# The order of the last pair's products in a fused QKV projection, and its last block stored in two halves

## The chip, the cores and the metric

The kernel runs on one core of a Trainium2 chip. The metric is the device time of one execution in microseconds; the figure given is the median of several runs. A profiled execution has a time of its own and a span, which goes from its first to its last instruction.

## What is computed

The reference multiplies a batch of activations by one weight matrix and splits the result into three parts, all in float32:

```python
batch, seq, hidden = 16, 512, 768
qkv = np.matmul(x, w_qkv)          # x (16, 512, 768), w_qkv (768, 2304)
q = qkv[..., :hidden]; k = qkv[..., hidden:2*hidden]; v = qkv[..., 2*hidden:]
return np.stack([q, k, v], axis=0).astype(np.float32)
```

So 8192 rows of x times 2304 columns of w, with 768 as the inner dimension. The output is 75.5 MB.

## The kernel before

**Tiles.** The 8192 rows are worked in 32 groups of 256 rows, two row blocks of 128 each (a group is `p`, and NP is 32). The 2304 columns are four blocks of 512 and a remainder of 256 (`CB`, `REM`). Two column blocks and two row blocks make a "quad": a 2 by 2 arrangement of 128x512 output blocks c11, c12, c21, c22. Quad `a` of a group has the first two column blocks (`q` is 0), quad `b` the last two (`q` is 1); the remainder columns lie between them, at 1024 to 1279, and belong to the middle third of the output.

**Products.** A quad is not computed as eight half products (two row blocks, two column blocks, two halves of the inner dimension) but as seven, by the Winograd form of Strassen's algorithm. Each product is three matmuls of 128x128 by 128x512 (line 258, in `product`). Products 1 and 2 use x and w rounded to bfloat16; products 3 to 7 use sums of blocks of x (made by GpSimd, `sums_x`) and of w (made once). In this text a6 is product 6 of quad a, and so on.

**Banks and readers.** A product is summed into a PSUM bank, and the block that it contributes to is read from there. The order inside `do` matters here:

- product 1 goes into bank x, and ScalarE copies it to c11 (line 267);
- product 2 goes into bank z, and VectorE adds it to c11 (line 280);
- product 6 is summed on top of product 1 in bank x, and ScalarE copies the sum to c12 (line 286);
- product 5 goes into bank y, and in the last group ScalarE copies it to c22 (line 291);
- product 7 is summed on top in bank x, and in the last group VectorE adds the sum to c22 (line 295);
- product 4 is summed on top in bank x, and ScalarE copies the sum to c21 (line 301);
- product 3 is summed on top in bank y, and VectorE adds the sum to c12 (line 304).

So products 6, 7 and 4 must each wait until the reader of the former sum in bank x is done, and product 3 until the reader of bank y is. A block is complete, and can be stored, after product 2 (c11), 7 (c22), 4 (c21) and 3 (c12).

**The remainder.** One row block of the 256 remainder columns is six matmuls of 128x128 by 128x256 (line 321, `rem_row`). In the last group, `rem_stored` makes one row block, copies its first 128 columns with ScalarE (line 423) and its other 128 with VectorE (line 424), and issues its store from ScalarE's DMA queue (line 426). In this text r0 and r1 are the remainders of the last group's two row blocks.

**Order.** The schedule is written out by hand: each engine executes its instructions in the order in which the program issues them (`manual_schedule`), and the semaphores between engines follow from the data. After a start-up in which the weights are loaded, rounded and summed, groups are worked two by two in the loop at the end of the kernel; the last group stands alone in `last`, which is where the change is made. Stores go to the DMA queue of SP, apart from the remainder's and one block (c21 of quad a), which go to ScalarE's. `store_cols` (line 416) stores one 128x512 block, 256 KB; where a block crosses from one third of the output to another, it is still one transfer.

Of the kernel before, what the change touches and what calls it, by code (L numbers as in the profile page):

```python
# [10 lines left out]
def kernel(  # L11
# [20 lines left out]
    nc = tc.nc  # L32
# [10 lines left out]
    CB = 512  # L43
    REM = N3 - 4 * CB
# [5 lines left out]
    ident = mybir.ActivationFunctionType.Identity  # L50
    add = mybir.AluOpType.add
# [188 lines left out]
    def quad(p, q, pool=o_pool, tag="o"):  # L240
        u = Quad()
        u.p, u.q = p, q
        u.o = pool.tile([P, 2, 2 * CB], fp32, name="o", tag=tag)
        u.x = u.y = u.z = None
        return u

    def product(u, n, ps, start):
        t1, t2, t3, t4 = ts[u.q]
        if n <= 2:
            h = (n - 1) * KH  # L250
            lhs = [xb[u.p][:, h + j, :P] for j in range(KH)]
            rhs = [b1[u.q][:, h + j, :] for j in range(KH)]
        else:
            k, t = {3: (4, b22[u.q][:]), 4: (0, t4), 5: (1, t1), 6: (2, t2), 7: (3, t3)}[n]
            lhs = [sr[u.p][:, k, j, :] for j in range(KH)]
            rhs = [t[:, j, :] for j in range(KH)]
        for j in range(KH):
            nc.tensor.matmul(  # L258
                ps[:], lhs[j], rhs[j],
                start=(start and j == 0), stop=(j == KH - 1), skip_group_check=True,  # L260
            )

    def bank():
        return ps_pool.tile([P, CB], fp32, name="ps")

    def evacuate(u):
        nc.scalar.activation(u.o[:, 0, :CB], u.x[:], ident)

    def do(u, n, out=True):
        c11, c12 = u.o[:, 0, :CB], u.o[:, 0, CB:]  # L270
        c21, c22 = u.o[:, 1, :CB], u.o[:, 1, CB:]
        if n == 1:
            u.x = bank()
            product(u, 1, u.x, True)
            if out:
                evacuate(u)
        elif n == 2:
            u.z = bank()
            product(u, 2, u.z, True)
            nc.vector.tensor_tensor(c11, c11, u.z[:], op=add)  # L280
        elif n == 6:
            first = u.x is None
            if first:
                u.x = bank()
            product(u, 6, u.x, first)
            nc.scalar.activation(c12, u.x[:], ident)  # L286
        elif n == 5:
            u.y = bank()
            product(u, 5, u.y, True)
            if u.p == NP - 1:  # L290
                nc.scalar.activation(c22, u.y[:], ident)
        elif n == 7:
            product(u, 7, u.x, False)
            if u.p == NP - 1:
                nc.vector.tensor_tensor(c22, c22, u.x[:], op=add)
            else:
                nc.scalar.activation(c22, u.x[:], ident)  # L297
                nc.vector.tensor_tensor(c22, c22, u.y[:], op=add)  # L298
        elif n == 4:
            product(u, 4, u.x, False)  # L300
            nc.scalar.activation(c21, u.x[:], ident)  # L301
        elif n == 3:
            product(u, 3, u.y, False)
            nc.vector.tensor_tensor(c12, c12, u.y[:], op=add)  # L304
# [14 lines left out]
    def rem_row(p, r, ps):  # L319
        for j in range(KT):  # L320
            nc.tensor.matmul(  # L321
                ps, xb[p][:, j, r * P:(r + 1) * P], w_rem[j // KH][:, j % KH, :],
                start=(j == 0), stop=(j == KT - 1), skip_group_check=True,
            )
# [77 lines left out]
    def store_cols(u, r, lo, hi, eng):  # L402

        c = Q_OFF[u.q] + lo
        n = hi - lo
        row = (2 * u.p + r) * P
        src = u.o[:, r, lo:hi]
        left = (c // H + 1) * H - c
        if left >= n:
            dst = out_flat[c // H, row:row + P, c % H:c % H + n]  # L410
        else:
            assert 2 * left == n
            first = out_flat[c // H, row:row + P, c % H:H]
            dst = bass.AP(first.tensor, first.offset, [[H, P], [M * H - H + left, 2], [1, left]])
            src = src.rearrange("m (s n) -> m s n", s=2)
        eng.dma_start(dst, src)

    def rem_stored(p, r):
        ps = bank()
        rem_row(p, r, ps[:, :REM])  # L420
        o = or_pool.tile([P, 2, REM], fp32, name="orem")
        half = REM // 2
        nc.scalar.activation(o[:, 0, :half], ps[:, :half], ident)  # L423
        nc.vector.tensor_copy(out=o[:, 0, half:], in_=ps[:, half:REM])  # L424
        row = (2 * p + r) * P
        nc.scalar.dma_start(out_flat[1, row:row + P, R_OFF - H:R_OFF - H + REM], o[:, 0, :])

    def last(a, b):

        do(a, 1)  # L430
        do(b, 1)
        rem_stored(a.p, 0)
        for u in (a, b):
            do(u, 2)
            store_cols(u, 0, 0, CB, nc.sync)
        do(a, 6)
        do(b, 6)
        for u in (a, b):
            do(u, 5)
            do(u, 7)  # L440
            store_cols(u, 1, CB, 2 * CB, nc.sync)
        for u in (a, b):
            do(u, 4)
            store_cols(u, 1, 0, CB, nc.scalar if u is a else nc.sync)
            do(u, 3)
            store_cols(u, 0, CB, 2 * CB, nc.sync)
        rem_stored(a.p, 1)


# [130 lines left out]
    u = quad(2, 0)  # L580
# [72 lines left out]
    for p in range(ND + 3, NP - 1, 2):  # L653
# [14 lines left out]
        a, b = quad(p, 0), quad(p, 1)  # L668
# [3 lines left out]
        plain(a, b, c, d, early, lambda: rem(c.p)()(), final)  # L672
        summed(c, d, {} if final else {0: lambda: transpose(p + 3, 2, 0)}, "parts" if final else True)
    last(quad(NP - 1, 0), quad(NP - 1, 1))


# [28 lines left out]
```

## Time and profile before

| | us |
|---|---|
| Median of 3 runs | 359.17 (358.98 to 359.32) |
| Profiled execution, its own time | 358.81 |
| Its span, first to last instruction | 357.0 |
| TensorE busy in the span | 350.6 |
| First matmul of the last group's stage in the record | 343.00 |
| End of the last matmul | 353.69 |
| Last store issued | 354.35 |

The remaining 1.81 us of the profiled execution's time lie outside its span. Engines are named PE (TensorE's matmuls), PEld (TensorE's weight loads), DVE (VectorE), ACT (ScalarE), POOL (GpSimd) and SP (which issues DMAs). Lines such as L304 are lines of the kernel. A line of the timeline has the start, the length, the engine, the line, the operation, what is written and read, the shapes and the number of instructions merged, and in brackets the idle time ahead of it with what ended that. The matmuls are pipelined, so the lengths of neighbours overlap; the distance between starts is what one costs. SPq and ACTq are the DMA queues of SP and ScalarE.

### The profile page before, as it was taken

Reading aid. Unit: us, or ns where it says so; the run is one execution under the profiler, and the core shown is the slowest. Engines: PE = TensorE matmul, PEld = TensorE weight load, DVE = VectorE, ACT = ScalarE, POOL = GpSimd, SP = SyncE. Lnnn points to the kernel's source line nnn. Section 1 sums busy time; section 2 is a strip of 40 time slices with the busy share of each in tenths; the row PEclk is TensorE's granted clock in tenths of the full one; section 3 lists DMA queues with packets and bytes.
Section 4 is the critical chain, followed back from the end, with each engine's and each line's share of the span. In section 5 each row is a group of like instructions: output and inputs, shape, how many; then the busy total and the mean of one; then the engine's idle time right before and its main releaser. Section 6 shows DMA issues by size and latency. Waiting matters only on the chain.

```text
span 357.0 us, 5315 instructions
## 1 busy us (share of the span) xinstructions
PE 350.6 (98%) x1757; PEld 252.1 (71%) x1776; DVE 264.4 (74%) x310; ACT 185.0 (52%) x317; POOL 177.3 (50%) x184
## 2 busy tenths in 40 slices
PE   7999999999999999999999999999999999999996
PEld 3474677768677686877768677686877768677674
DVE  3789876796877869777695877869777695876743
ACT  4587754545454553645545454553645545454553
POOL 0031773376566453665535566353665535566320
PEclk9999999999999999999999999999999999999999
DMA  7997999999999898998979899698999979887497
GB/s 296 380 353 238 325 378 340 373 317 348 308 311 340 257 361 206 347 266 285 361 197 385 227 342 307 209 402 213 347 263 307 331 196 392 225 303 280 155 380 260
DMA packets 82075, 108.10 MB, mean 303 GB/s; under 512 B 4992, under 2 KB 62080, under 8 KB 82048
## 3 DMA queue, kind: packets, MB, share of 16 engines
q1 hardware_dynamic: 75088, 102.52, 85.7%
q10 hardware_dynamic: 6960, 5.24, 5.5%
q8 instruction: 14, 0.23, 0.3%
q14 instruction: 13, 0.11, 0.1%
HBM read 32.24 MB, written 75.50 MB: 302 GB/s over the span
## 4 chain that ended last, share of the span: by engine, by line
PE 74%; POOL 15%; DVE 6%; issue 3%; DMA 2%; ACT 0%; SPq 0%
PE ps L258 56%; PE ps L321 12%; PE ps L496 6%; DVE xf L155 6%; POOL xb L205 5%; POOL s L226 3%; POOL s L225 3%; POOL s L227 3%; DMA xin<-in_x_dram 2%; PE ps L185 0%; DVE o L304 0%; ACT xc L166 0%; SPq L162 0%; DVE orem L424 0%; ACT orem L423 0%
## 5 line engine op out<-in xcount | busy, mean ns | idle before, releaser
L258 PE MATMUL ps<-t,s 128*128 128x512 f32 x720 | 177.9, 395 | 0.0
L258 PEld LDWEIGHTS ps<-t,s 128*128 128x128 f32 x720 | 135.1, 188 | 29.5
L155 DVE STREAM_TRANSPOSE xf<-xin 128x768 f32<-128x768 f32 (+1 forms) x45 | 93.3, 2075 | 4.3 <-DMA xin<-in_x_dram 4.3
L258 PE MATMUL ps<-b,xb 128*128 128x512 bf16 x343 | 81.6, 379 | 1.1
L298 DVE TENSOR_TENSOR o<-o,ps 128x512 f32<-128x512 f32 x56 | 38.5, 688 | 50.7 <-ACT o L297 50.0
L205 POOL CAST xb<-xf 128x1536 bf16<-128x1536 f32 x28 | 41.1, 1467 | 56.9 <-DVE xf L155 54.8
L225 POOL TENSOR_TENSOR s<-xf 128x384 fp32r<-128x384 f32 x29 | 31.0, 1068 | 72.9 <-DVE xf L155 71.1
L258 PEld LDWEIGHTS <-xb 128*128 128x128 bf16 x360 | 33.9, 98 | 36.7 <-issue 3.9
L304 DVE TENSOR_TENSOR o<-o,ps 128x512 f32<-128x512 f32 x60 | 41.1, 687 | 20.5 <-PE ps L258 19.4
L297 ACT ACTIVATE o<-ps 128x512 f32<-128x512 f32 x56 | 33.5, 598 | 42.1 <-PE ps L258 42.1
L258 PE MATMUL ps<-b,s 128*128 128x512 f32 x180 | 50.6, 389 | 0.0
L301 ACT ACTIVATE o<-ps 128x512 f32<-128x512 f32 x60 | 35.9, 598 | 25.2 <-PE ps L258 22.8
L378 DVE TENSOR_TENSOR o<-o,ps 128x512 f32<-128x512 f32 x78 | 47.8, 680 | 0.0
L321 PE MATMUL ps<-w_rem,xb 128*128 128x256 bf16 x384 | 47.4, 273 | 0.0
L286 ACT ACTIVATE o<-ps 128x512 f32<-128x512 f32 x60 | 35.9, 599 | 19.4 <-PE ps L258 14.0
L321 PEld LDWEIGHTS <-xb 128*128 128x128 bf16 x384 | 37.3, 98 | 11.5 <-issue 0.5
L335 ACT ACTIVATE orem<-ps 128x512 f32<-128x512 f32 x31 | 18.5, 598 | 48.3 <-PE ps L321 34.0
L258 PEld LDWEIGHTS ps<-b,s 128*128 128x128 f32 x180 | 33.8, 188 | 7.0
L226 POOL TENSOR_TENSOR s<-s,xf 128x384 fp32r<-128x384 f32 x29 | 29.5, 1018 | 2.3
L227 POOL TENSOR_TENSOR s<-xf 128x384 fp32r<-128x384 f32 x29 | 29.4, 1015 | 0.0
L229 POOL TENSOR_TENSOR s<-xf,s 128x384 fp32r<-128x384 f32 x29 | 29.2, 1008 | 0.0
L382 ACT ACTIVATE o<-ps 128x512 f32<-128x512 f32 x26 | 15.5, 598 | 17.9 <-PE ps L258 17.3
(49 smaller groups left out, 161.2 us busy)
## 6 DMA issues: line engine op xcount, KB each, us to landing
out_dram<-o SPq DMA_DIRECT2D x60, 768.0 KB, 4.6
out_dram<-o SPq DMA_DIRECT2D x75, 256.0 KB, 3.8
xin<-in_x_dram SPq DMA_DIRECT2D x88, 192.0 KB, 5.6
out_dram<-orem SPq DMA_DIRECT2D x31, 256.0 KB, 2.2
xin<-in_x_dram ACTq DMA_DIRECT2D x24, 192.0 KB, 4.4
st<-in_w_qkv_dram SPq DMA_DIRECT2D x5, 768.0 KB, 7.9
xin<-in_x_dram SPq DMA_DIRECT2D x2, 768.0 KB, 4.9
st<-in_w_qkv_dram SPq DMA_DIRECT2D x6, 256.0 KB, 6.0
```

The costliest lines, as they stand in the source:

```text
L155: nc.vector.transpose(turned[:, g:g + n], rows[:, g:g + n])
L205: nc.gpsimd.tensor_copy(out=xb[p][:], in_=xf[p][:])
L225: 1: lambda g: g.tensor_tensor(s[:, 1], a21, a22, op=add),
L226: 2: lambda g: g.tensor_tensor(s[:, 2], s[:, 1], a11, op=sub),
L227: 3: lambda g: g.tensor_tensor(s[:, 3], a11, a21, op=sub),
L258: nc.tensor.matmul(ps[:], lhs[j], rhs[j], start=(start and j == 0), stop=(j == KH - 1), skip_group_check=True,)
L286: nc.scalar.activation(c12, u.x[:], ident)
L298: nc.vector.tensor_tensor(c22, c22, u.y[:], op=add)
L301: nc.scalar.activation(c21, u.x[:], ident)
L304: nc.vector.tensor_tensor(c12, c12, u.y[:], op=add)
L321: nc.tensor.matmul(ps, xb[p][:, j, r * P:(r + 1) * P], w_rem[j // KH][:, j % KH, :], start=(j == 0), stop=(j == KT - 1), skip_group_check= ...
L378: dve.tensor_tensor(c, c, u.z[:], op=add)
```

## The change

Only the last group is touched. In `rem_stored`, one ScalarE copy of 256 columns takes the place of two copies of 128 columns by ScalarE and VectorE. In `last`, the order of the blocks of work on TensorE changes:

- before: a1 b1 r0 a2 b2 a6 b6 a5 a7 b5 b7 a4 a3 b4 b3 r1
- after: a1 b1 a2 b2 a6 a5 a7 b6 b5 a4 a3 b7 r0 b4 b3 r1

Quad a's blocks are all done before b7, r0, b4 and b3. All block stores are issued from SP, in the order c22, c21, c12 of a, then c22, c21, c12 of b. The very last block, c12 of b, is added by VectorE in two halves of 256 columns, and each half is stored by its own 128 KB transfer as soon as it is added. The matmuls themselves are the same ones.

```diff
@@ rem_stored
-        half = REM // 2
-        nc.scalar.activation(o[:, 0, :half], ps[:, :half], ident)
-        nc.vector.tensor_copy(out=o[:, 0, half:], in_=ps[:, half:REM])
+        nc.scalar.activation(o[:, 0, :], ps[:, :REM], ident)
@@ last
         do(a, 1)
         do(b, 1)
-        rem_stored(a.p, 0)
         for u in (a, b):
             do(u, 2)
             store_cols(u, 0, 0, CB, nc.sync)
-        do(a, 6)
-        do(b, 6)
-        for u in (a, b):
-            do(u, 5)
-            do(u, 7)
-            store_cols(u, 1, CB, 2 * CB, nc.sync)
-        for u in (a, b):
-            do(u, 4)
-            store_cols(u, 1, 0, CB, nc.scalar if u is a else nc.sync)
-            do(u, 3)
-            store_cols(u, 0, CB, 2 * CB, nc.sync)
+        for u, n in ((a, 6), (a, 5), (a, 7), (b, 6), (b, 5)):
+            do(u, n)
+        store_cols(a, 1, CB, 2 * CB, nc.sync)
+        do(a, 4)
+        store_cols(a, 1, 0, CB, nc.sync)
+        do(a, 3)
+        store_cols(a, 0, CB, 2 * CB, nc.sync)
+        do(b, 7)
+        store_cols(b, 1, CB, 2 * CB, nc.sync)
+        rem_stored(a.p, 0)
+        do(b, 4)
+        store_cols(b, 1, 0, CB, nc.sync)
+        product(b, 3, b.y, False)
+        for lo in range(0, CB, CB // 2):
+            hi = lo + CB // 2
+            c12 = b.o[:, 0, CB + lo:CB + hi]
+            nc.vector.tensor_tensor(c12, c12, b.y[:, lo:hi], op=add)
+            store_cols(b, 0, CB + lo, CB + hi, nc.sync)
         rem_stored(a.p, 1)
```

## The prediction, made before the changed kernel was run

> **What bounds the kernel now.** I read the page first, then the last microseconds of the chain that ended last, then the timeline there, then the DMA windows. The page shows TensorE busy for nearly the whole span at the full granted clock, so a change in the last pair is worth what it does to the end of TensorE's stream and to the tail behind it.
>
> ```profile
> span 357.0 us, 5315 instructions
> PE 350.6 (98%) x1757; PEld 252.1 (71%) x1776; DVE 264.4 (74%) x310; ACT 185.0 (52%) x317; POOL 177.3 (50%) x184
> PEclk9999999999999999999999999999999999999999
> ```
>
> The chain (start, length, what) is TensorE without a gap from 344.90 to 353.69, then ScalarE's and VectorE's halves of the last remainder, one after the other:
>
> ```profile
> 344.90 8.11 PE ps L258 x36
> 353.01 0.69 PE ps L321 x6
> 353.69 0.02 issue
> 353.71 0.29 ACT orem L423
> 354.00 0.02 issue
> 354.02 0.29 DVE orem L424
> ```
>
> The timeline (start, length, engine, line) shows how products and evacuations interlock. A product of three matmuls starts every 0.68 us (351.49, 352.17, 352.85). Its weight loads start 0.22 us ahead of its matmuls (351.26, 351.94). The evacuation of a product starts 0.20 us after the first matmul of the next one (351.69, 352.36, 353.05).
>
> ```profile
> 351.26 0.64 PEld L258 LDWEIGHTS ps<-t,s 128*128 128x128 f32 x3
> 351.49 0.84 PE L258 MATMUL ps<-t,s 128*128 128x512 f32 x3
> 351.69 0.69 DVE L304 TENSOR_TENSOR o<-o,ps 128x512 f32<-128x512 f32 x1 [0.60 <-PE ps L258]
> 351.94 0.64 PEld L258 LDWEIGHTS ps<-b,s 128*128 128x128 f32 x3
> 352.17 0.84 PE L258 MATMUL ps<-b,s 128*128 128x512 f32 x3
> 352.36 0.60 ACT L301 ACTIVATE o<-ps 128x512 f32<-128x512 f32 x1 [0.76 <-PE ps L258]
> 352.85 0.83 PE L321 MATMUL ps<-w_rem,xb 128*128 128x256 bf16 x6
> 353.05 0.69 DVE L304 TENSOR_TENSOR o<-o,ps 128x512 f32<-128x512 f32 x1 [0.67 <-PE ps L258]
> 354.35 0.34 ACTq L426 DMA_DIRECT2D out_dram<-orem  x1
> ```
>
> From the windows (engines' busy time, then clock, DMA share, GB/s): the DMA engines are mostly idle from 349.5 to 352.0, then full, so four block stores come in a burst at the end. The landing times of the remainder's two stores are 3.8 us in the crowd and 1.8 us (1.83 before rounding) for the last.
>
> ```profile
> 349.50:352.00 2.50, 2.50 (x13) 2.07 (x12) 1.22 (x3) 1.20 (x2) 0.00 (x0) 1.00 0.39 138
> 352.00:355.50 3.50, 1.68 (x11) 1.01 (x9) 1.35 (x3) 0.87 (x2) 0.00 (x0) 1.00 1.04 385
> DMA to landing us min/median/max: 1.8/2.8/3.8
> ```
>
> **The change, part by part.** TensorE issues the same matmuls, so its work is unchanged; what counts is waits. A product that accumulates into a bank may start only when the reader of that bank's previous value has finished. Before, two other products lay between every such pair in the last stage; I go through the new order a1 b1 a2 b2 a6 a5 a7 b6 b5 a4 a3 b7 r0 b4 b3 r1 (r is a remainder row) with s for the start of the block that lies between.
>
> First hold, a6 to a7: a7 accumulates into the bank that ScalarE copies after a6, and only a5 lies between. The copy runs from s+0.20 for 0.60 us, to s+0.80. A hand-over costs 0.03 to 0.04 us (ACT ends 353.99, DVE starts 354.02; DVE ends 354.31, the store is issued 354.35), so a7's weights may load at s+0.84. Unheld they would load at s+0.68-0.22 = s+0.46. TensorE stands for 0.38 us.
>
> Second hold, b7 to b4: VectorE adds b7 into c22, and only the moved r0 lies between. The add runs from s+0.20 for 0.69 us, so b4's weights may load at s+0.93. The nearest row for a product behind a remainder row is earlier in the run: remainder at 43.81, next weights at 44.37, that is s+0.56. The hold is 0.37 us. The add of a3 is just ahead of b7's on VectorE, but began 0.68 us earlier and lasts 0.69, which moves this by 0.01.
>
> ```profile
> 43.38 0.69 DVE L519 TENSOR_TENSOR o<-o,ps 128x512 f32<-128x512 f32 x1 [1.08 <-PE ps L258]
> 43.81 0.83 PE L321 MATMUL ps<-w_rem,xb 128*128 128x256 bf16 x6
> 44.37 0.30 PEld L258 LDWEIGHTS ps<-t,s 128*128 128x128 f32 x2
> ```
>
> The same rows check it: there the reader started at 43.38 and ended at 44.07, with a product and a remainder before its successor's weights at 44.37. That is 0.30 us to spare; with 0.68 us of cover removed it is 0.38 short. Behind each held load stands all the rest of TensorE's stream, and every later evacuation and store waits with it. The other pairs keep two blocks: a7's add ends about 1.6 us after a7 while b6 and b5 run, and b6's copy has b5, a4 and a3 before b7. Sum on TensorE: +0.75 us, none of it covered, since TensorE already runs to 353.69 without a gap.
>
> Moving r0 from third place to thirteenth also moves its copy and its store on ScalarE's DMA queue; the queue is then issuing for 0.34 to 0.38 us between the copies of a4 and b4, which are over 2 us apart, so this costs nothing. The a21 store goes from ScalarE's queue to SP's, where the stores are now in the order in which they come ready, each issue taking about 0.37 us of the 0.68 between blocks: nothing as well.
>
> Last remainder: one ScalarE copy of 256 columns replaces 0.28 us on ScalarE, 0.29 on VectorE and the hand-overs, 0.64 us from 353.71 to the issue at 354.35. The trace has no 256-column copy; it lies between 0.28 us (128 columns) and 0.60 (512), on the line between them 0.39, and I take that: 0.42 to the issue, a gain of 0.22 us (bounds 0.33 and 0.01). The issue comes at 354.35+0.75-0.22 = 354.88.
>
> Last block in two halves: a half add lies between a 128-column copy (0.29) and the whole add (0.69); I take 0.42. The adds start at 353.05+0.75 = 353.80, the halves are stored at about 354.25 and 354.67, where the whole was stored at 353.76 (+0.75 is 354.51). So the half order costs 0.16 us for the last half, but it is issued ahead of the remainder's store and decides nothing unless the transfers queue. I therefore check the queue: from b21's store (352.99+0.75 = 353.74) four transfers of 640 KB, 655 kB, have to go. At 385 GB/s this takes 1.70 us. An unqueued 256 KB store lands 2.0 us after its issue and its bytes take 0.68, so 1.3 us are outside the transfer; the burst lands at 353.74+1.30+1.70 = 356.74. The remainder by itself lands at 354.88+1.83 = 356.71. Before, it landed at 354.35+1.83 = 356.18. The later of the two counts: +0.56 us. The 0.8 us from there to the end of the span stay.
>
> The profiled execution took 358.81 us, 0.36 below the median of the runs; its sum is 359.37, and on the median 359.73. I forecast 359.7 us: a loss, but a small one. 0.2% is 0.72 us, about what a measurement of this kernel can tell from no change.
>
> **The rivals.** First, the weights could be loaded while TensorE is held, so that only the matmul waits. The load is 0.19 us in the rows, so each hold shrinks by that: 0.56-0.38 = +0.18, 359.35 us. Against it: where TensorE waits for ScalarE, in the transposes at the start, the list of waits books 1.9 us on the loads and 0.6 on the matmuls, so it is the load that is held. The Trainium skill says this is possible: TensorE: Matmul & The Clock Gate, section "Step-by-step: what each phase is for", lets TensorE pull weight loads ahead of running matmuls. By that rule the time is this rival's 359.35; the trace agrees that loads run ahead of matmuls, but shows none running ahead of its own wait.
>
> Second, slower beyond the bound: restarting TensorE after a hold costs more than the held time, because the load no longer lies beside a matmul. The trace has no hold inside the steady stream; the nearest price is again the load, 0.19 us more per hold, as in the first rival and of the other sign: +0.94, 360.1 us. It decides from 0.08 us per hold on (0.56+0.16 = 0.72).
>
> Third, faster: the holds do not arise and only the shorter evacuation remains: 0.22 us gained, 358.95 us; at the best bound 0.33, 358.84. For this an evacuation would have to start and end 0.4 us sooner than any row shows. Even so it stays inside the bound.
>
> **How the numbers follow.** Chances: forecast 0.58, weights ahead 0.17, costly restart 0.18, no holds 0.07. Slower by over 0.2% is the restart rival and the upper part of the forecast (0.12), in which the copy or the half adds take their upper bounds: 0.30. Faster by over 0.2% needs the third rival and run-to-run spread: 0.03. The rest, 0.67, lies within. The range from 359.1 to 360.2 holds the forecast, the first rival and most of the second; alone, the forecast's range is 359.5 to 359.9.
>
> **What would show it.** In the changed trace: a gap in TensorE of about 0.38 us between a5 and a7, ended by ScalarE's copy of line 286, and one of 0.37 us between r0 and b4, ended by VectorE's add of line 295; the last remainder's matmuls ending near 354.4; its copy at about 0.39 us; the last store issued near 354.9; DMA busy from about 350 on instead of 352. I am wrong if the gaps are missing or of another size, or if the last landing is set by a store queue longer than 640 KB.

## The result, and the profile after

| | before | after |
|---|---|---|
| Median of 17 runs, us | 359.0 (358.79 to 359.48) | 359.65 (359.56 to 360.0) |
| Ratio | 1 | 1.0016 (95% interval 1.0009 to 1.0023) |
| Profiled execution: its time, its span, us | 358.81, 357.0 | 359.84, 358.1 |
| Last matmul of r1 starts after the mark, us | 9.72 | 10.61 |
| Last store issued after the mark, us | 10.66 | 11.33 |
| Last landing after the mark, us | 12.50 | 13.29 |
| End of the span after the mark, us | 13.34 | 14.13 |

The changed kernel is 0.65 us slower, where +0.56 was forecast. The span of the profiled execution grew by more, 1.04 us, but 0.25 us of that lie ahead of the last group: the first copy of line 267 in that group, which I use as the mark, starts at 343.68 before and at 343.93 after, though nothing ahead of it was changed. From the mark to the end the difference is 0.79 us, and that is what the traces are compared by here. Times after the mark and times of landing are taken from the trace to the nanosecond; the views round them.

The granted clock is full, as before. The chain that ended last in the changed kernel (start, length, what; most pieces under 0.05 us are left out) is no longer TensorE alone: after 15 matmuls it passes through two adds of VectorE. The short piece between them, DVEq, is an instruction on VectorE's queue that belongs to b7's add and only waits.

```profile
344.92 2.26 PE ps L258 x10
347.18 0.09 issue
347.27 3.68 PE ps L258 x15
350.98 0.69 DVE o L304
351.66 0.02 DVEq L295
351.73 0.70 DVE o L295
352.47 1.67 PE ps L258 x6
354.14 0.68 PE ps L321 x6
354.85 0.38 ACT orem L422
```

The timeline of the changed kernel shows the two holds. The first: a6's copy (line 286) runs from 346.52 to 347.12, and the weights of a7 load at 347.24, after 0.50 us in which no weights were loaded. The record names no releaser there, but the load stands behind that copy; in e8 below, where the wait is longer, the record names it.

```profile
346.33 1.87 PE L258 MATMUL ps<-t,s 128*128 128x512 f32 x6
346.52 0.60 ACT L286 ACTIVATE o<-ps 128x512 f32<-128x512 f32 x1 [1.35 <-PE ps L258]
347.24 0.76 PEld L258 LDWEIGHTS ps<-t,s 128*128 128x128 f32 x4 [0.50 <-issue]
```

The second: r0 starts at 351.46, b7's add (line 295) runs from 351.73 to 352.42, and b4's weights load at 352.47, 1.01 us after r0's start, where 0.56 is the distance without a wait. Here the releaser is named.

```profile
351.46 0.83 PE L321 MATMUL ps<-w_rem,xb 128*128 128x256 bf16 x6
351.73 0.69 DVE L295 TENSOR_TENSOR o<-o,ps 128x512 f32<-128x512 f32 x1
352.32 0.39 ACT L422 ACTIVATE orem<-ps 128x256 f32<-128x256 f32 x1 [1.43 <-PE ps L321]
352.47 0.53 PEld L258 LDWEIGHTS ps<-t,s 128*128 128x128 f32 x3 [0.46 <-DVE o L295]
352.47 0.98 PE L258 MATMUL ps<-t,s 128*128 128x512 f32 x3 [0.18 <-DVE o L295]
```

The windows of the changed kernel (engines' busy time, then clock, DMA share, GB/s) show what stands in the place of one full stretch of stores: an almost idle half microsecond, at 55 GB/s, while b4 and its copy are late, and then a last burst. By the packets the pause is 0.54 us. It is shorter, 0.27 and 0.14 us, in the variants e3 and e9 below, which have no hold, and the kernel before has none there.

```profile
350.00:352.50 2.50, 2.32 (x15) 1.54 (x13) 1.38 (x2) 0.99 (x3) 0.00 (x0) 1.00 0.57 212
352.50:354.60 2.10, 2.10 (x12) 1.52 (x12) 0.42 (x2) 0.81 (x2) 0.00 (x0) 1.00 0.86 312
354.60:355.10 0.50, 0.21 (x2) 0.00 (x0) 0.33 (x1) 0.25 (x1) 0.00 (x0) 1.00 0.15 55
355.10:357.00 1.90, 0.00 (x0) 0.00 (x0) 0.00 (x0) 0.13 (x1) 0.00 (x0) 1.00 0.95 331
```

### The profile page after: what moved, and what is told of

The parts are those of the page before. It is cut to its first block, busy times and chain, and to the rows that moved or that the text cites. A ratio compares the mean times of both kernels' runs of the same rounds, so it can differ in the third digit from the quotient of the medians.

```text
span 358.1 us, 5335 instructions
## 1 busy us (share of the span) xinstructions
PE 352.9 (99%) x1776; PEld 252.1 (70%) x1776; DVE 263.9 (74%) x309; ACT 185.3 (52%) x317; POOL 177.6 (50%) x184
## 4 chain that ended last, share of the span: by engine, by line
PE 97%; DMA 1%; DVE 1%; ACT 0%; issue 0%; DVEq 0%
PE ps L258 79%; PE ps L321 12%; PE ps L500 6%; DMA xin<-in_x_dram 1%; PE ps L185 1%; DVE o L295 0%; DVE o L304 0%; ACT xc L166 0%; ACT orem L422 0%; DVE xb L194 0%; DVE xc L165 0%; DVEq L295 0%
## 5 line engine op out<-in xcount | busy, mean ns | idle before, releaser
L258 PE MATMUL ps<-b,xb 128*128 128x512 bf16 x360 | 85.2, 379 | 0.0
```

The lines of the kernel that those rows point to most:

```text
L258: nc.tensor.matmul(ps[:], lhs[j], rhs[j], start=(start and j == 0), stop=(j == KH - 1), skip_group_check=True,)
```

## The experiments

Eleven further kernels were run, one of them (e1, again as e11) twice. The table gives the median against the kernel before on the same chip, the ratio with its interval, and from the trace, in us after the mark, the start of the last matmul and the end of the span.

| run | median minus before, us | ratio (95%) | last matmul | end |
|---|---|---|---|---|
| before | 0 | 1 | 9.72 | 13.34 |
| after | +0.65 | 1.0016 (1.0009 to 1.0023) | 10.61 | 14.13 |
| e1, no first hold | +0.48 | 1.0012 (1.0003 to 1.0021) | 10.26 | 13.79 |
| e2, no second hold | +0.58 | 1.0017 (1.0008 to 1.0025) | 10.15 | 13.94 |
| e3, no holds | +0.25 | 1.0007 (0.9999 to 1.0016) | 9.81 | 13.58 |
| e4, one copy alone | -0.07 | 0.9999 (0.9990 to 1.0008) | 9.72 | 13.33 |
| e5, halves alone | +0.05 | 1.0002 (0.9993 to 1.0010) | 9.72 | 13.38 |
| e6, e3 with a whole last block | +0.09 | 1.0003 (0.9994 to 1.0012) | 9.81 | 13.48 |
| e9, e3 with r0's store from SP | +0.07 | 1.0002 (0.9993 to 1.0011) | 9.81 | 13.39 |
| e10, remainders last | -0.14 | 0.9996 (0.9987 to 1.0005) | 9.76 | 13.19 |
| e7, first hold twice, in before | +0.72 | 1.0018 (1.0009 to 1.0027) | 10.38 | 13.99 |
| e8, nothing between a6 and a7 | one time, 360.12 (before 358.83) | | 10.85 | 14.63 |
| e12, e10 with both from SP | -0.21 | 0.9993 (0.9984 to 1.0002) | 9.76 | 13.04 |

One of e1's eleven executions took 1291.73 us, for a reason not known, and it was the profiled one, so the trace values in e1's row are from e11, the same kernel run once more (one time, 359.33, before 358.83). In all rows but that of the changed kernel (0.65 and 0.79), the difference of the medians and that of the ends agree within 0.09 us.

### Taking the holds away: e1, e2, e3

The products of the changed kernel are put in another order, so that two blocks or more lie between the two products of the hold that is taken away. Every block and store remains.

```diff
-a6 a5 a7 b6 b5 a4 a3 b7 r0 b4 b3 r1     (after)
+a6 b6 a5 a7 b5 a3 a4 b7 r0 b4 b3 r1     (e1)
+a6 a5 a7 b6 b5 a4 b7 a3 r0 b4 b3 r1     (e2)
+a6 b6 a5 a7 b5 a3 b7 a4 r0 b4 b3 r1     (e3)
```

> Against the kernel before the changed one is +0.65 us. Order a6 b6 a5 a7 b5 a3 a4 b7 r0 b4 b3: two blocks now lie between a6 and a7, and b7's add no longer stands behind a3's on VectorE; b7 to b4 is still one block apart. Theory of the holds: the gap before a7 (0.34 us lost) is gone, the gap before b4 shrinks from about 0.45 to 0.39, so about +0.25 against the kernel before. Rival, the store queue at the end decides: the same four transfers of 640 KB come last, so still about +0.6.

> Order a6 a5 a7 b6 b5 a4 b7 a3 r0 b4 b3: a3 and r0 now lie between b7 and b4, the gap before a7 stays. Theory of the holds: 0.45 us come back, about +0.2 against the kernel before. Rival of the store queue: about +0.6, as the last 640 KB are the same.

> Order a6 b6 a5 a7 b5 a3 b7 a4 r0 b4 b3: both pairs two blocks apart or more, the rest as in the changed kernel. Theory of the holds: only the shorter evacuation of the last remainder is left, -0.2 against the kernel before (between 0 and -0.35). Rival of the store queue: still about +0.5. Rival of the restarts (TensorE loses more than the held time): -0.2 as well, but then the loss in the changed trace must exceed the two gaps.

TensorE confirms the holds to a few hundredths: against the changed kernel its last matmul comes 0.35 us earlier without the first, 0.46 without the second, 0.80 without both. The end did not follow all the way. Without the first hold it comes 0.34 us earlier, without the second only 0.19, and without both 0.55. By the medians alone e2, at +0.58, came out as the rival of the store queue had it and not as the holds did, and e1 and e3 lie between the two. With no hold left the kernel is still 0.25 us slower than before, not 0.2 faster. The interval just reaches 1, but in the trace the end is 0.24 us late as well, while TensorE is only 0.08 late.

The traces say where the rest went. b21's store is issued 0.35 us earlier than in the changed kernel in e11, 0.32 in e2 and 0.67 in e3, and the last landing comes 0.34, 0.30 and 0.65 earlier. So in e2 and e3 about 0.14 us of what TensorE gained are lost ahead of that store, and 0.10 more between the last landing and the end of the span: 0.94 us there, where it is 0.84 in e11 and in the changed kernel. The first loss is shown next, the second under e10. So the holds are real, and they are not the whole of the answer.

The trace of e3 shows one thing that the holds had covered: ScalarE issues r0's store from 352.37 to 352.75, and only then copies b4 (352.79). In the variants without the second hold b4 is ready by then and waits, 0.14 us.

```profile
351.96 0.38 ACT L422 ACTIVATE orem<-ps 128x256 f32<-128x256 f32 x1
352.37 0.38 ACTq L424 DMA_DIRECT2D out_dram<-orem  x1
352.45 0.86 PE L258 MATMUL ps<-b,s 128*128 128x512 f32 x3
352.79 0.60 ACT L301 ACTIVATE o<-ps 128x512 f32<-128x512 f32 x1 [0.45 <-PE ps L258]
```

### One copy in place of two: e4

```diff
-        nc.scalar.activation(o[:, 0, :half], ps[:, :half], ident)
-        nc.vector.tensor_copy(out=o[:, 0, half:], in_=ps[:, half:REM])
+        nc.scalar.activation(o[:, 0, :], ps[:, :REM], ident)
```

> The kernel before with the remainder evacuated in one 256-column copy on ScalarE, nothing else changed. Theory of the holds: the last store is issued 0.22 us sooner; -0.2 us if its own latency sets the end, less if it then queues behind the 256 KB of b3's block (whose store is issued at 353.76 and landed at 355.84): between -0.25 and -0.05. Rival of the store queue: 0.0, the end is set by bytes and not by the issue.

The rival holds, by the trace; the times cannot tell, since -0.07 with an interval of about 0.3 us to either side fits both. The last store was issued 0.22 us sooner after the mark (10.45 in place of 10.66), and the last landing stayed (12.495 and 12.497). What the store gained it lost in the queue: the least time from issue to landing of the remainder's stores is 2.0 us here, where it was 1.8. In both traces r1's first packet moves 0.83 to 0.84 us ahead of its landing, and 0.15 us before the last packet of b12's store, which is on the other queue, has ended. It waits 0.99 us from its issue to that first packet in the kernel before and 1.22 in e4, and 0.90 in e10, where fewer bytes are queued ahead of it. So the end of the kernel before is set by queued bytes, not by the last remainder's own chain. The last steps of e4 in its timeline:

```profile
353.70 0.38 ACT L422 ACTIVATE orem<-ps 128x256 f32<-128x256 f32 x1 [0.75 <-PE ps L321]
354.11 0.34 ACTq L424 DMA_DIRECT2D out_dram<-orem  x1
```

The landing times of the remainder's two stores in e4, from the view of line 424:

```profile
DMA to landing us min/median/max: 2.0/2.7/3.4
```

### The halves and the queue: e5, e6, e9

e5 is the kernel before with only the last block halved, e6 is e3 with the last block whole, e9 is e3 with r0's store issued from SP. The cut shows the edits in short form.

```diff
@@ e5, and the reverse of it in e6
-        do(b, 3)
-        store_cols(b, 0, CB, 2 * CB, nc.sync)
+        product(b, 3, b.y, False)
+        for lo in range(0, CB, CB // 2):
+            hi = lo + CB // 2
+            c12 = b.o[:, 0, CB + lo:CB + hi]
+            nc.vector.tensor_tensor(c12, c12, b.y[:, lo:hi], op=add)
+            store_cols(b, 0, CB + lo, CB + hi, nc.sync)
@@ e9, where rem_stored takes the engine that issues its store
-        rem_stored(a.p, 0)
+        rem_stored(a.p, 0, nc.sync)
```

> The kernel before with only its last block added and stored in two halves. Theory now held, the end is set by the bytes that are queued from b21's store on, and b4's copy decides when that queue starts: two 128 KB transfers in place of one of 256 KB cost what they cost the queue, 0.0 to +0.15 us against the kernel before (640 KB took 1.87 us in halves where 1.70 was worked out for whole blocks). Rival, the last remainder's own chain sets the end: 0.0, since that chain is untouched.

> The variant without gaps (a6 b6 a5 a7 b5 a3 b7 a4 r0 b4 b3 r1, measured +0.25 us against the kernel before) with its last block added and stored whole. Theory of the queue: the halves' share, up to 0.15 us, comes back: +0.10 to +0.25. Rival of the last remainder's chain: no change, +0.25.

> The variant without gaps, with r0's store issued from SP in place of ScalarE. In that variant's trace ScalarE issues r0's store from 153.82 to 154.19 while b4's product is ready for its copy at 154.10, and the copy starts at 154.24, 0.14 us late. Theory of the queue: b21's store and the 640 KB behind it come 0.14 us earlier: about +0.1 against the kernel before. Rival of the last remainder's chain: unchanged, +0.25.

The times in e9's expectation are counted from another zero: in the trace shown above, ScalarE issues r0's store from 352.37 to 352.75, b4's product is ready for its copy at 352.65, and the copy starts at 352.79.

e6 and e9 came out on the side of the queue: +0.09 and +0.07 us, where the last remainder's own chain would have left +0.25. In e5 the times cannot tell (+0.05), but in its trace r1's store is issued at the same time after the mark and lands 0.04 us later, so its landing hangs on the bytes ahead of it. The halves cost 0.05 us at the end of the kernel before, and in e3 their removal gives 0.10 in the trace (0.06 up to the last landing, 0.04 behind it) and 0.16 between the medians. Moving r0's store off ScalarE gives 0.19 us in the trace and 0.18 between the medians: 0.15 up to the last landing, as the 0.14 for which b4's copy had waited, and 0.04 behind it. By the times alone e6, e9 and the kernel before cannot be told apart.

### How much cover a hold wants, and what it costs elsewhere: e7, e8, e11

e7 makes the first hold in the kernel before, for both quads; e8 takes the last block of cover away in e3.

```diff
-a6 b6 a5 a7 b5 b7      (before)
+a6 a5 a7 b6 b5 b7      (e7)
-a6 b6 a5 a7 b5         (e3)
+b6 a5 a6 a7 b5         (e8)
```

> The kernel before with one change of order: a6 a5 a7 b6 b5 b7 in place of a6 b6 a5 a7 b5 b7, so that one block lies between product 6 and product 7 of both quads. Remainders, stores and the last block stay as they were. Theory of the holds: two gaps of 0.34 us each on TensorE, which delay all that follows, also the queue of the last stores: +0.6 to +0.7 us against the kernel before. Rival, that a gap this early in the last group is made good by the idle time of the DMA engines around it: 0.0 to +0.3.

> The variant without gaps (+0.25 us), with a6 moved so that it stands directly ahead of a7 (b6 a5 a6 a7). Theory of the holds: one block less of cover than in the changed kernel costs one block's time more, so the gap at a7 is 0.34+0.68 = 1.02 us, and the end about 1.0 us later than in the variant without gaps. If the copy could overlap the product that accumulates on it, the gap would be about 0.3.

> The same kernel as e1_no_hold1, for a trace of it (that run's profiled execution was an outlier of 1291.73 us). The add of b7 now follows a4's copy and not a3's add: theory, the gap before b4 is 0.39 us in place of 0.45, and the gap before a7 is gone. Rival: the gap stays 0.45, then the queue on VectorE is not what made it larger than the 0.37 forecast.

e7: the last matmul is 0.65 us late, the end 0.65, the median 0.72. A hold that has nine blocks of TensorE's work behind it is paid in full; the idle DMA engines around it gave nothing back. e8: 1.05 us late on TensorE and 1.05 at the end, against e3, so without any cover the hold is 1.03 us (from where a7 starts in e3 to the start of b5 are 1.71 us, where 0.68 is the pace), one block's time longer than the 0.34 with one block between, as worked out. TensorE's own line shows it waiting for the copy:

```profile
348.44 1.62 PE L258 MATMUL ps<-t,s 128*128 128x512 f32 x6 [0.78 <-ACT o L286]
```

e11: the rival holds. With no add of a3 ahead, b4's weights still come 1.00 us after r0's start (350.94 to 351.94), as in the changed kernel. The reason is in the start of the add: 0.26 us after r0's first matmul (351.20).

```profile
350.94 0.83 PE L321 MATMUL ps<-w_rem,xb 128*128 128x256 bf16 x6
351.20 0.69 DVE L295 TENSOR_TENSOR o<-o,ps 128x512 f32<-128x512 f32 x1 [0.74 <-PE ps L258]
351.94 0.53 PEld L258 LDWEIGHTS ps<-t,s 128*128 128x128 f32 x3 [0.46 <-DVE o L295]
```

The kernel before had it too: this is its timeline at b7's add, which waits for two engines, TensorE and ScalarE's copy of c22. It starts 0.27 us after the first matmul of the next product (a4, 350.12), not 0.20.

```profile
350.12 0.62 PE L258 MATMUL ps<-t,s 128*128 128x512 f32 x2
350.39 0.69 DVE L295 TENSOR_TENSOR o<-o,ps 128x512 f32<-128x512 f32 x1 [0.67 <-PE ps L258]
```

That the second wait makes the difference, and not the line, e8 shows: there a6's copy comes later than a5's, a3's add of line 304 has a waiting instruction of its own ahead of it too, which it has in no other trace, and it starts 0.27 us after the next product (350.59 to 350.86).

### A better order: e10, e12

If queued bytes set the end, the blocks with half the bytes for the same TensorE time, the remainders, belong at the end. e10 does this with two blocks or more between any such pair; e12 also issues r1's store from SP. Both keep the single copy of a remainder and store the last block whole.

```diff
-a6 b6 a5 a7 b5 a3 b7 a4 r0 b4 b3 r1     (e3, e9)
+a6 b6 a5 b5 a7 b7 a3 a4 b4 b3 r0 r1     (e10, e12)
```

> Order a6 b6 a5 b5 a7 b7 a3 a4 b4 b3 r0 r1, last block whole, r0's store from SP: no pair nearer than two blocks, and both remainders, which have half the bytes of a block for the same TensorE time, at the very end, so that the queue can drain under them. Theory of the queue: the end comes down to the last remainder's own chain, whose store would be issued near 0.2 us sooner than in the kernel before and no longer queue: -0.2 to -0.4 us against the kernel before. Rival, TensorE's end alone counts: about 0.0.

> The order with the remainders last (-0.14 us), with r1's store also issued from SP, so that its semaphore is the last in the order in which SP looks at them. In the traces the span ends 0.84 us after the last landing when that semaphore is the last in the order, and 0.97 us in the order with the remainders last. Theory: 0.1 us gained, about -0.25 us against the kernel before. Rival: SP's order of waits is not what makes the difference, -0.14.

e10's median, -0.14, lies between the theory and its rival, and its interval holds both, so the trace has to tell. There TensorE ends 0.03 us later than before and yet the last landing is 0.28 us earlier: r1's store now takes 1.74 us from issue to landing (1.83 before, 2.05 in e4). But the end is only 0.15 earlier: after the last landing SP looks at the semaphores of the last stores in a fixed order, and here the last to land was not the last in the order. Two looks follow it, 0.06 us each; in e6 one look follows, and there it is 0.90 us from the last landing to the end. The list of SP's waits (waiting line, what it waited for, us in total, times, longest) shows it for e10: one wait of 1.3 us for a remainder's store comes before the looks at others that have landed by then.

```profile
SPq L700 <- DMA out_dram<-orem: 1.3, 1, 1.3
SPq L700 <- DMA out_dram<-o: 0.5, 1, 0.5
```

In the same list of e12 the waits are short, in the order in which the stores land:

```profile
SPq L700 <- DMA out_dram<-orem: 0.6, 2, 0.3
SPq L700 <- DMA out_dram<-o: 0.6, 1, 0.6
```

From the last landing to the end of the span it is 0.965 us in e10 and 0.839 in e12, as in the kernel before, and e12 ends 0.29 us sooner than that. Its median is 0.21 us below the kernel before; the interval still touches 1, so it is the fastest kernel in the traces and not shown to be faster in the times. It is faster than the changed kernel: their ratios to the kernel before, each taken on its own chip, have intervals that do not meet.

## Why the prediction was right, and where not

The direction, the size and the place came out: two holds on TensorE, of 0.34 and 0.46 us where 0.38 and 0.37 were worked out, 0.80 in place of 0.75 together; e1, e2, e3, e7 and e8 show them one by one. The number alone would not have shown it, since the range up to 360.2 held two rivals as well, and that 0.56 came so near to 0.65 is in part luck: several terms were off and partly made up for each other. Nor was 0.72 us what these measurements can just tell from no change; with 17 runs of each kernel the interval of the ratio was 0.0007 to either side, 0.25 us. Point by point:

- **First hold, 0.38, was 0.34.** The weights came 0.11 us after the copy's end, not 0.04, but the first matmuls after the hold followed their loads more closely and made up 0.11 us. The rival of the costly restart falls with this. So does that of the weights ahead, since the held loads at 347.24 and 352.47 stand behind their wait. The Trainium skill (TensorE: Matmul & The Clock Gate, section "Step-by-step: what each phase is for") has loads pulled ahead of running matmuls. The trace agrees with that in the steady stream, where a load starts 0.22 us ahead.
- **Second hold, 0.37, was 0.46.** The step that failed is the start of b7's add: I took 0.20 us after the next block's start from the adds of line 304, where line 295's own row in the trace of before had 0.27. The row of line 519 that I used as a check has it too: that add starts at 43.38, 0.27 us after the product at 43.11. With 0.27, 0.69 and 0.05 for the hand-over, less 0.56, it is 0.45. I had looked to the a3 add ahead of it; e11 shows that it has no part.
- **The pace of the new order** was left out. The last matmul was 0.89 us late, 0.08 more than the two holds, and the same 0.08 stand in e3, which has no hold. There the first three products after the switch from bfloat16 take 0.89, 0.69 and 0.69 us, where they took 0.88, 0.68 and 0.68 before; that is 0.03 us, and e10 is late by that much. The rest comes from r0 in its new place: b4 behind it takes 0.78 us and b3 0.70, where 0.68 is the pace. Why is not shown.
- **The single copy, a gain of 0.22, gained nothing.** The copy took 0.38 to 0.39 us and the issue came as much sooner as forecast, but e4 shows that in the kernel before the last store already waited behind b12's bytes. The step that failed is "Before, it landed at 354.35+1.83": I took 1.83 for a transfer without a queue, though the windows showed the DMA engines full until 355.5. In e10, with fewer bytes ahead of it, the same store took 1.74. It did little harm to the sum, because the later of two landings counted there, and that was the burst's, by 0.03 us.
- **The tail, b21's store and the 640 KB behind it,** was the right chain. b21's store was forecast 0.75 us later than before and was 0.87 later, by the longer holds and the pace; from its issue to the last landing 3.00 us were forecast and 3.11 measured, since the burst took 1.87 us and not 1.70. These two, 0.12 and 0.11, are the 0.23 between the 0.56 forecast and the 0.79 of the trace. The median, with 0.65, lies between; why it is 0.14 below the trace is not settled.
- **The half order, "0.16 us for the last half", deciding nothing unless transfers queue:** they do queue, and the halves' part is 0.05 us (e5) to 0.10 (e6 against e3).
- **The sign "DMA busy from about 350 on instead of 352"** did not come: from 350.0 to 352.5 the share is 0.57 (first window above), with the engines full only from about 351.9 on, and the pause of 0.54 us was not foreseen. The queue at the end was not longer than the 640 KB forecast: 655,616 bytes move between the pause and the last packet.
- **r0's store on ScalarE's queue, "costs nothing",** was true only under the second hold; without that it costs 0.14 to 0.19 us (e3, e9).

Not settled is why the last group's mark lay 0.25 us later in this profile than in that of before. In the other traces it lies between 343.67 and 344.08, without a pattern that follows the change, and the medians agree with the distances from the mark better than with the spans.

## What to carry to other kernels

When products are reordered, list for each accumulation the reader that must finish first, and count what lies between: its start, its length and the hand-over, against the cover of the blocks between and the lead of the weight load, with the reader's own row and not that of a like one. A hold on a full TensorE was paid in full in e7 and e8; taking one away gave less where another delay behind it came to light (e2, e3). Where the DMA engines are full at the end of a kernel, ask which bytes are still queued before counting on a shorter last step, and try the blocks with the fewest bytes for their compute time last; here that brought the last landing forward by 0.28 us, and a gain in the times is not shown.

## What the runs showed that was not expected

- An add that waits for two engines starts about 0.07 us later than one that waits for one: 0.26 to 0.27 against 0.20 us after the next block's first matmul (line 295 against 304, and line 304 in e8 against the other traces).
- A DMA issue on ScalarE occupied it for 0.34 to 0.41 us, and the copy behind it waits: b4's copy came 0.14 us late in e3.
- The order in which SP looks at the last semaphores moves the end by up to 0.13 us after the same last landing: 0.84 us from landing to end where the last to land is the last in the order (before, after, e12 and others), 0.90 in e6 and e9, 0.94 to 0.97 in e2, e3, e8 and e10.
- Cutting the last 256 KB into two transfers did not bring the end forward at all, neither in the kernel before (e5) nor in the one without holds (e6 against e3).
